# A two-layer trunk on one core: block products over neighbouring token chunks, their sums made in the first layer and kept in DRAM, and the rope of two chunks stacked

## The chip, the cores and the metric

The kernel runs on one core of one Trainium2 chip. The metric is the device time of one execution in microseconds (us). The time before is the median of three runs, 2751.1 us (2750.38 to 2755.59). One further execution was taken with the hardware profiler; the profile below is of that one.

The engines are called as the profile calls them: PE is the matrix engine (PEld its weight loads), DVE the vector engine, ACT the scalar engine, POOL the gpsimd engine, and SP the engine whose queue starts nearly all transfers. Each engine works through its own queue in order.

## The reference, cut to what matters

There are two pre-norm residual layers on 2048 tokens of width 1024. The first mixes with gated linear attention, the second with three groups of dilated windowed attention. Each layer also attends to a memory of 256 rows.

```python
h = rmsnorm(x, norm_w[i])                       # per layer
mix, q_mem, gate = gla_mixer(...) if i == 0 else dilated_mixer(...)
mem_o = memory_attention(q_mem, mem_n, w_memkv[i])
x = x + (concat([mix, mem_o]) * silu(gate)) @ w_out[i]

# dilated_mixer, layer 1: six heads of 128 in each of three groups
for g, (window, dil) in enumerate(((128, 1), (512, 4), (2048, 16))):
    qkv = (h @ w_in[:, base:base + 3 * MIXER_WIDTH]).reshape(B, T, 3, 6, 128)
    q, k = partial_rope(qkv[:, :, 0], pos), partial_rope(qkv[:, :, 1], pos)   # first 32 of 128
    o, lse = dilated_group(q, k, qkv[:, :, 2], window, dil)
o = sum over g of softmax(lse)[g] * o[g]
rest = h @ w_in[:, 9 * MIXER_WIDTH:]            # queries of the memory, gate
```

Everything is in 32-bit floats. The kernel reaches that precision with pairs of 16-bit floats, a high and a low part of each number, and three matmuls for each product (hi·hi, hi·lo, lo·hi; the helper `mm3`, L179 to L181).

## The kernel before, in words

The hidden state of the second layer, transposed, is the tile `h2T`: 128 partitions, a high and a low part, eight slices of the width, 2048 tokens. A *projection* (`proj_t`) multiplies it with 128 columns of a weight for a *chunk* of 512 tokens: 24 matmuls of 128x512 into one PSUM bank. Banks for this come in rotation from three (`mm_bank`: two of the pool ps_mm, one of ps_x). The stages, by the trace:

- **First layer, first part (0 to 458 us):** the projections and the chunked recurrence.
- **First layer, second part (458 to 906 us):** a loop over 16 blocks of 128 tokens, some 28 us each. One pass has the memory's attention, the gate and the output projection of a block (`a2_q`, `a2_gate`, `a2_out`; its results leave their banks at L683), and for the block before it the norm and its transposition into `h2T` (`a2_h2`, L697 and L698). The second layer's first weights are loaded meanwhile.
- **Pre-stage (906 to 1040 us):** twelve projections, eight for the queries of the memory (`memq`, read out at L953 to L957) and four for one part of the gate (`gate4`, read out at L999 to L1003). Between them in program order stand the loading, scaling and splitting of the first set of weights (`set_raw`, `set_norm`, `set_diff`, `set_split`; L873 to L883) and six of the eight calls of `sums`.
- **Block products (1040 to 1466 us):** twelve sets of weights. Each is multiplied by the 2x2-block scheme with seven products instead of eight (`sblock`). The token side of the 2x2 is the first half of the tokens against the second, the other side the two halves of the width. Three of the seven need sums of the four quarters of `h2T`, in the SBUF tiles S1, S2 and S4; a fourth, S3 = A11 − A21, overwrites the quarter A21 in `h2T`. Copies of A21 (`a21_d`, in DRAM) are put back at the end. `sums(x)` makes S1, S2, S4 and for x below 4 also S3 for a slice of 128 tokens of each half: L828 adds a high and a low part, L839 to L845 combine them, L832 (ACT) and L833 split the result again. The last two calls and the other four S3 run within the first set (`late`).
- **Heads (1470 to 2526 us):** 18 heads of eight steps each. A step has one projection: q or k (e even or odd) of chunk e // 2, then the scores of ten steps earlier (`att_scores`) and the products with v of thirteen steps earlier (`att_pv`). After each odd step `rope_pair` (L1127 to L1144) turns q and k of the chunk: ACT copies the 32 rows to be turned of both banks to SBUF (L1133), DVE swaps halves (L1134), POOL and DVE multiply with the tables (L1135, L1136), DVE adds them back into the banks (L1138), and ACT and DVE write the high and the low part (L1141, L1142). L1142 is the last reader of the bank. In four of each 24 steps `item_mix` (L1286 to L1300) weighs and adds the three groups of a finished head, by two multiplications on POOL (L1289, L1294) and the rest on DVE.
- **Tail (2526 to 2741 us):** the last heads, the output projection and the final norm.

A Tile scheduler puts the instructions of DVE, ACT, POOL and SP into queues, by a simulation of the program. In the second layer PE's order is the program's.

## Time and profile before

| | |
|---|---|
| median of three runs | 2751.1 us |
| the profiled execution's own time | 2743.19 us |
| its span in the trace | 2741.4 us |
| mean granted clock of PE | 0.971 |
| PE busy | 2546.4 us (93%) |
| DVE busy | 1642.0 us (60%) |
| ACT busy | 1311.6 us (48%) |
| POOL busy | 649.2 us (24%) |
| moved by DMA | 337.13 MB, mean 123 GB/s |

Busy time is the time in which an engine executes. For PE the records overlap: a matmul of 128x512 stands in the trace with some 380 ns, though the next one starts 207 ns later. A row of the groups has line, engine, operation, output and input tiles with shape and type, count, then busy time in us and mean ns of one, then idle time of the engine just before it and what ended it. A row of the waits has who waited, for which instruction, the sum in us, the count and the longest. A row of the windows has the stretch, its length, busy time and count of each engine, the granted clock of PE, and the share and rate of DMA.

### The profile page before, as it was taken

What the parts mean: (1) busy time and instruction counts of PE and PEld (TensorE: products, weight loads), DVE (VectorE), ACT (ScalarE), POOL (GpSimd) and SP (SyncE); (2) the same over time, 40 slices, a digit from 0 to 9 for tenths busy, and PEclk for the clock granted to TensorE, in tenths of its full rate; (3) what the DMA queues carried; (4) which work ended last, traced back from release to release, by engine and by line L of the source; (5) the groups of instructions that cost most, each with busy time, mean ns of one, the idle gap of its engine ahead of it and who ended that gap; (6) DMA issues with size and microseconds to landing.
All of it is one profiled execution on the core that took longest, in us unless ns stands there. A gap on an engine that the chain in (4) does not pass through costs nothing.

```text
span 2741.4 us, 45032 instructions
## 1 busy us (share of the span) xinstructions
PE 2546.4 (93%) x17137; PEld 1699.6 (62%) x17137; DVE 1642.0 (60%) x3483; ACT 1311.6 (48%) x2921; POOL 649.2 (24%) x513
## 2 busy tenths in 40 slices
PE   7989999999999959999999999799897998978899
PEld 6879998888998524544444455354453544534798
DVE  6345444655655696655655566757657576676643
ACT  6356444544444446555645455354454444535232
POOL 0000000000001254555441222423323233242200
PEclk9999999999999989999999999899998999998899
DMA  6241113342334214767754144645547446366642
GB/s 212 82 133 71 64 56 109 103 103 82 108 88 122 73 51 129 179 168 187 168 149 145 37 99 113 182 98 137 129 118 185 96 118 148 99 190 154 182 148 102
DMA packets 517837, 337.13 MB, mean 123 GB/s; under 512 B 348834, under 2 KB 460916, under 8 KB 515316
## 3 DMA queue, kind: packets, MB, share of 16 engines
q1 hardware_dynamic: 517620, 334.26, 44.5%
q8 instruction: 134, 2.20, 0.3%
q14 instruction: 83, 0.68, 0.1%
HBM read 179.45 MB, written 89.57 MB: 98 GB/s over the span
## 4 chain that ended last, share of the span: by engine, by line
PE 69%; DVE 12%; DMA 9%; issue 4%; ACT 3%; POOL 2%; SPq 1%; DVEq 0%; POOLq 0%; ACTq 0%
PE ps_mm L179 14%; PE ps_mm L180 13%; PE ps_mm L181 13%; PE ps_x L179 5%; PE ps_x L181 5%; PE ps_x L180 5%; DMA fb<-fd 3%; DMA stg<-in_w_in_b 2%; PE ps_tr L166 1%; PE ps_o L181 1%; PE ps_o L180 1%; PE ps_o L179 1%; DMA pt<-ph 1%; DVE ps_mm L1138 1%; DVE fb L1297 1%
## 5 line engine op out<-in xcount | busy, mean ns | idle before, releaser
L179 PE MATMUL ps_mm<-h2T,w 128*128 128x512 f16 x1112 | 435.7, 392 | 67.8 <-DVE q L1142 65.1
L180 PE MATMUL ps_mm<-h2T,w 128*128 128x512 f16 x1112 | 435.6, 392 | 2.7 <-POOL h2T L833 2.7
L181 PE MATMUL ps_mm<-h2T,w 128*128 128x512 f16 x1112 | 434.1, 390 | 0.0
L180 PEld LDWEIGHTS <-w 128*128 128x128 f16 x1952 | 194.2, 99 | 325.0 <-issue 124.7
L179 PE MATMUL ps_mm<-w,hT 128*128 128x256 f16 (+1 forms) x1408 | 387.5, 275 | 4.3 <-ACT v L488 1.3
L180 PE MATMUL ps_mm<-w,hT 128*128 128x256 f16 (+1 forms) x1408 | 386.4, 275 | 0.0
L181 PE MATMUL ps_mm<-w,hT 128*128 128x256 f16 (+1 forms) x1408 | 384.8, 275 | 0.4 <-DVE hT L382 0.4
L181 PEld LDWEIGHTS <-w 128*128 128x128 f16 x1952 | 194.6, 100 | 244.9 <-issue 23.7
L179 PEld LDWEIGHTS <-w 128*128 128x128 f16 x1952 | 194.4, 100 | 241.3 <-issue 19.4
L1182 ACT ACTIVATE pm<-pm,st,cols 128x256 f32<-128x256 f32 (+1 forms) x288 | 156.7, 545 | 265.1 <-DVE st L1177 260.6
L173 POOL TENSOR_TENSOR ph<-pm,ph 128x512 f16<-128x512 f32 (+2 forms) x144 | 154.8, 1075 | 481.7 <-ACT ph L172 369.4
L179 PE MATMUL ps_x<-h2T,w 128*128 128x512 f16 x552 | 211.9, 384 | 38.9 <-DVE q L1142 21.7
L173 POOL TENSOR_TENSOR stg<-mp,stg 128x512 f16<-128x512 f32 x16 | 18.5, 1159 | 834.9 <-DMA ogd<-og 459.1
L181 PE MATMUL ps_x<-h2T,w 128*128 128x512 f16 x552 | 211.7, 383 | 0.0
L180 PE MATMUL ps_x<-h2T,w 128*128 128x512 f16 x552 | 211.7, 383 | 0.0
L1173 DVE CUSTOM_DVE_ANT_0 pm<-ps_g,mw 128x256 f32<-128x256 f32 (+1 forms) x288 | 93.5, 360 | 153.1 <-PE ps_g L181 152.1
L179 PEld LDWEIGHTS <-hT 128*128 128x128 f16 x1408 | 138.8, 99 | 24.2 <-issue 5.6
L180 PEld LDWEIGHTS <-hT 128*128 128x128 f16 x1408 | 138.7, 99 | 24.2 <-issue 6.0
L1135 POOL TENSOR_TENSOR rw<-rw,rope 64x512 f32<-64x512 f32 x72 | 96.2, 1336 | 228.6 <-DVE rw L1134 210.8
L181 PEld LDWEIGHTS <-hT 128*128 128x128 f16 x1408 | 139.2, 99 | 17.8 <-DVE hT L382 0.7
L1133 ACT ACTIVATE rx<-ps_mm 32x512 f32<-32x512 f32 x96 | 56.1, 584 | 113.2 <-PE ps_mm L181 109.6
L179 PE MATMUL ps_o<-pt,v 128*128 128x128 f16 (+1 forms) x384 | 75.7, 229 | 9.7 <-DVE rw L1211 3.7
(448 smaller groups left out, 6064.9 us busy)
## 6 DMA issues: line engine op xcount, KB each, us to landing
stg<-in_w_in_b SPq DMA_DIRECT2D x80, 256.0 KB
v<-vd SPq DMA_DIRECT2D x18, 1024.0 KB
fb<-fd SPq DMA_DIRECT2D x24, 768.0 KB
od<-osb SPq DMA_DIRECT2D x68, 256.0 KB
og<-od SPq DMA_DIRECT2D x68, 256.0 KB
x<-in_x SPq DMA_DIRECT2D x32, 512.0 KB
stg<-in_w_in_b SPq DMA_DIRECT2D x24, 512.0 KB
vd<-vo SPq DMA_DIRECT2D x48, 256.0 KB
```

The lines of the kernel that those rows point to most:

```text
L166: PE.transpose(t[:, (k - k0) * P:(k - k0 + 1) * P], src[:, k * P:(k + 1) * P], ident)
L173: G.tensor_tensor(out=lo, in0=src, in1=hi, op=ALU.subtract)
L179: PE.matmul(o, sh, mh, start=first, stop=False)
L180: PE.matmul(o, sh, ml, start=False, stop=False)
L181: PE.matmul(o, sl, mh, start=False, stop=last)
L1133: A.activation(out=X[32 * j:32 * j + 32, :], in_=ts[j][0:32, :], func=AF.Copy)
L1135: G.tensor_tensor(out=W, in0=W, in1=rt[1], op=ALU.mult)
L1138: V.tensor_tensor(out=ts[j][0:32, :], in0=X[32 * j:32 * j + 32, :], in1=W[32 * j:32 * j + 32, :], op=ALU.add)
L1173: V.tensor_tensor_reduce(out=pm[:, at:at + w * P], in0=s[:, at:at + w * P], in1=masks["mw" if w == 2 else "mf"], scale=1.0, scalar=NEG, op ...
L1182: A.activation(out=p_, in_=p_, func=AF.Exp, scale=sc, bias=st[:, jc + jj:jc + jj + 1], accum_out=st[:, ns + jc + jj:ns + jc + jj + 1])
L1297: V.tensor_tensor(out=acc, in0=acc, in1=fb[:, 2], op=ALU.add)
```

## The change

There are three parts.

**Neighbouring chunks.** The token side of the 2x2 is now chunk c against chunk c + 1 (512 tokens each) for c = 0 and 2, in place of the first half against the second. The tiles S1, S2, S4 are laid out by slices of 128 tokens, so that a product that uses them reads four runs of 128 for its 512 columns.

**Sums in the first layer.** With this pairing a slice of sums needs blocks b and b + 4 of 128 tokens, and can be made while the first layer still runs. `a2_sums` does so after the blocks in `SUMS_AT` for six of the eight slices, S3 too, and stores them in DRAM (`s_d`). One call has three instructions on POOL, ten on DVE, four on ACT and four transfers of 256 KB. The last call has one buffer for its four outputs, the others four. In the pre-stage `load_s` and `load_s3` bring them back (6 MB together) on SP's queue, and only the sums 6 and 7 are made there; the first set has none. The order of the twelve projections changes to chunks 1, 3, 0, 2 for the memory and 1, 3, 0, 2 for the gate.

**Rope of two chunks.** `evac` writes high and low parts of all 128 rows out of a bank without the turn, after copying its 32 rows into a quarter of the SBUF tile `rx`; after that the bank is free. When both chunks of a pair (0 and 2, then 1 and 3) are there, `rope_quad` does swap, multiplications, addition and split for all four quarters at once (128x512 in place of 64x512), and eight DVE copies of 32x512 put the turned rows over the others in q and k. It runs 36 times where `rope_pair` ran 72 times.

```diff
+SUMS_AT = (6, 8, 10, 12, 13, 14)
...
+        def a2_sums(i):
+            b = i // 4 * 8 + i % 4
+            (h11, l11), (h12, l12), (h21, l21), (h22, l22) = (
+                [h2T[:, hl, 4 * k:4 * k + 4, d * P:(d + 1) * P] for hl in range(2)] for d in (b, b + 4) for k in (0, 1))
...
+            def split(t, name, o, eng):
+                o = o.rearrange("p a (k n) -> p a k n", k=4)
+                A.activation(out=o[:, 0], in_=t, func=AF.Copy)
+                eng.tensor_tensor(out=o[:, 1], in0=t, in1=o[:, 0], op=ALU.subtract)
+                SY.dma_start(s_d[name][:, i], o)
+
+            G.tensor_tensor(out=x, in0=h21, in1=l21, op=ALU.add)
+            V.tensor_tensor(out=s, in0=h22, in1=l22, op=ALU.add)
+            V.tensor_tensor(out=s, in0=s, in1=x, op=ALU.add)
+            os_ = [ag[:, 3]] * 3 if i + 1 == len(SUMS_AT) else [as_[:, y] for y in (1, 2, 3)]
+            split(s, "S1", os_[0], V)
+            G.tensor_tensor(out=x, in0=h11, in1=x, op=ALU.subtract)
+            G.tensor_tensor(out=x, in0=x, in1=l11, op=ALU.add)
+            split(x, "S3", os_[1], V)
+            V.tensor_tensor(out=s, in0=s, in1=h11, op=ALU.subtract)
+            V.tensor_tensor(out=s, in0=s, in1=l11, op=ALU.subtract)
+            split(s, "S2", os_[2], V)
+            V.tensor_tensor(out=s, in0=h12, in1=s, op=ALU.subtract)
+            V.tensor_tensor(out=s, in0=s, in1=l12, op=ALU.add)
+            split(s, "S4", ag[:, 3], V)
...
             if b > 0:
                 a2_h2(b - 1, xt)
+                if b in SUMS_AT:
+                    a2_sums(SUMS_AT.index(b))
...
-        def quad(i, k, hl, ts):
-            return h2T[:, hl, 4 * k:4 * k + 4, i * H + ts.start:i * H + ts.stop]
+        def quad(i, k, hl, x, n=1):
+            t0 = x // 4 * 1024 + i * 512 + x % 4 * P
+            return h2T[:, hl, 4 * k:4 * k + 4, t0:t0 + n * P]
...
-                    mm3(o, wt[:, 0, k], wt[:, 1, k], hi[:, k], lo[:, k], k == 0, k == 3)
+                    if an in ops:
+                        mv, ov_ = [quad(*ops[an], x, cc * 4, 4)[:, k] for x in range(2)], o
+                    else:
+                        mv, ov_ = [Ss[an][:, cc * 4:cc * 4 + 4, x, k] for x in range(2)], o.rearrange(
+                            "p (a n) -> p a n", a=4)
+                    mm3(ov_, wt[:, 0, k], wt[:, 1, k], *mv, k == 0, k == 3)
...
-        memq(2)
-        out_q(0, 0, proj_t(wq["w"][0], 0))
+        load_s(slice(0, 4))
+        memq(1)
+        out_q(3, 0, proj_t(wq["w"][0], 3))
...
-        gate4(2)
-        sums(0)
-        sums(1)
-        gate4(0)
-        sums(2)
-        memq(1)
+        gate4(1)
+        for x in range(4):
+            load_s3(x)
+        gate4(3)
+        load_s(slice(4, 6))
+        for x in range(4, 6):
+            load_s3(x)
+        sums(6)
+        memq(0)
...
-    def rope_pair(ts, c, g, dsts):
+    def evac(ts, c, g, dsts, X):
         r0 = 64 * (c // 2)
         for j in range(2):
-            A.activation(out=X[32 * j:32 * j + 32, :], in_=ts[j][0:32, :], func=AF.Copy)
-        V.stream_shuffle(W, X, SWAP)
-        G.tensor_tensor(out=W, in0=W, in1=rt[1], op=ALU.mult)
-        V.tensor_tensor(out=X, in0=X, in1=rt[0], op=ALU.mult)
-        for j in range(2):
-            V.tensor_tensor(out=ts[j][0:32, :], in0=X[32 * j:32 * j + 32, :], in1=W[32 * j:32 * j + 32, :], op=ALU.add)
+            A.activation(out=X[r0 + 32 * j:r0 + 32 * j + 32, :], in_=ts[j][0:32, :], func=AF.Copy)
         for j in range(2):
             hi = gdst(dsts[j][:, 0, :], g, c)
             A.activation(out=hi, in_=perm(ts[j], g), func=AF.Copy, scale=SQ)
             V.scalar_tensor_tensor(out=gdst(dsts[j][:, 1, :], g, c), in0=perm(ts[j], g), scalar=SQ, in1=hi,
                                    op0=ALU.mult, op1=ALU.subtract)
+
+    def rope_quad(c, g, dsts, X):
+        cs = slice(c * 512, (c + 1) * 512)
+        W = tl(bk, [P, 512], F32, "rw")
+        V.stream_shuffle(W, X, SWAP)
+        G.tensor_tensor(out=W, in0=W, in1=rope[1][:, cs], op=ALU.mult)
+        V.tensor_tensor(out=X, in0=X, in1=rope[0][:, cs], op=ALU.mult)
+        V.tensor_tensor(out=W, in0=X, in1=W, op=ALU.add)
+        hl = X.bitcast(F16).rearrange("p (a n) -> p a n", a=2)
+        hi, lo = fold(hl[:, 0], g), fold(hl[:, 1], g)
+        A.activation(out=hi, in_=perm(W, g), func=AF.Copy, scale=SQ)
+        V.scalar_tensor_tensor(out=lo, in0=perm(W, g), scalar=SQ, in1=hi, op0=ALU.mult, op1=ALU.subtract)
+        for y in range(2):
+            for j in range(2):
+                r0 = 64 * y + 32 * j
+                for x in range(2):
+                    V.tensor_copy(gdst(dsts[j][0:32, x, :], g, c + 2 * y), fold(hl[r0:r0 + 32, x], g))
...
-        live[e % 2] = proj_t(d["w"][e % 2], e // 2)
+        c = (0, 2, 1, 3)[e // 2]
+        live[e % 2] = proj_t(d["w"][e % 2], c)
...
+        if e % 4 == 3:
+            rope_quad(c % 2, u[1], hds[n]["qk"], rx)
```

How the scheduler's queues change shows at three places. The numbers behind a tile's name tell its instances apart.

The first is DVE's queue at one mixing step of the heads. Before (rx and rw are the rope's tiles, fb and og the mixing's, osb a finished part of the attention's output, q and k the heads' operands, ps_x and ps_mm the projections' banks):

```order
L1134 STREAM_SHUFFLE rw_18712<-rx_18711 64x512
L1211 COPY osb_18749<-ps_o_18679 128x512
L1177 TENSOR_SCALAR st_2642_18307<-mx_18725,cols_88 128x2
L1136 TENSOR_TENSOR rx_18711<-rx_18711,rope_2382_16404 64x512
L1138 TENSOR_TENSOR ps_x_18625<-rx_18711,rw_18712 32x512
L1138 TENSOR_TENSOR ps_mm_18686<-rx_18711,rw_18712 32x512
L1291 TENSOR_TENSOR fb_18932<-og_18928,fb_18932 128x512
L1142 SCALAR_TENSOR_TENSOR q_18208<-ps_x_18625,q_18208 128x4x128
L1142 SCALAR_TENSOR_TENSOR k_18209<-ps_mm_18686,k_18209 128x4x128
L1297 TENSOR_TENSOR fb_18932<-fb_18932 128x512
```

After, at a mixing step of the same head (L1175 is the low part out of the bank, L1181 the rope's swap, L1341 to L1350 the mixing, L1223 the maxima of the scores):

```order
L1175 SCALAR_TENSOR_TENSOR q_18208<-ps_x_18621,q_18208 128x4x128
L1341 TENSOR_TENSOR fb_18654<-og_18650,fb_18654 128x512
L1347 TENSOR_TENSOR fb_18654<-fb_18654 128x512
L1348 TENSOR_TENSOR fb_18654<-fb_18654 128x512
L1223 ISA pm_18730,mx_18729<-ps_g_18728,mw_16386 128x128
L1223 ISA mx_18729 128x1
L1223 ISA pm_18730,mx_18729<-ps_g_18728,mw_16386 128x128
L1223 ISA mx_18729 128x1
L1181 STREAM_SHUFFLE rw_18713<-rx_18514 128x512
L1261 COPY osb_18753<-ps_o_18675 128x512
L1350 TENSOR_TENSOR sg_18648<-fb_18654,sg_18648 128x16x32
L1175 SCALAR_TENSOR_TENSOR k_18209<-ps_mm_18682,k_18209 128x4x128
```

The bank of q is now read out ahead of the mixing and with no rope ahead of it; the bank of k is read out ten instructions later, behind the mixing.

The second is DVE's queue in the last block of the first layer. Before (x is the block's output, ps_o and ps_x its banks, h2T the transposed hidden state):

```order
L683 SCALAR_TENSOR_TENSOR x_10909<-ps_o_10911,cj_10907,x_10909 128x256
L683 SCALAR_TENSOR_TENSOR x_10909<-ps_x_10962,cj_10907,x_10909 128x256
L698 TENSOR_TENSOR h2T_5111<-ps_tr_11022,h2T_5111 128x4x128
L774 CAST rb_1512_11232<-rm_11230 128x1
L698 TENSOR_TENSOR h2T_5111<-ps_tr_11029,h2T_5111 128x4x128
L683 SCALAR_TENSOR_TENSOR x_10909<-ps_o_10911,cj_10907,x_10909 128x256
L683 SCALAR_TENSOR_TENSOR x_10909<-ps_x_10962,cj_10907,x_10909 128x256
L692 SCALAR_TENSOR_TENSOR sg_11044<-x_10909,rs_1486_11041,nwb_850_5121 128x1024
```

After, with the last call of `a2_sums` (L719 takes the low part of a split, L730 to L734 combine; stg is the staging tile in which the sums lie):

```order
L687 SCALAR_TENSOR_TENSOR x_11011<-ps_o_11013,cj_11009,x_11011 128x256
L731 TENSOR_TENSOR stg_5333<-stg_5333,h2T_5115 128x512
L687 SCALAR_TENSOR_TENSOR x_11011<-ps_x_11064,cj_11009,x_11011 128x256
L702 TENSOR_TENSOR h2T_5115<-ps_tr_11131,h2T_5115 128x4x128
L719 TENSOR_TENSOR stg_5333<-stg_5333 128x512
L812 CAST rb_1488_11337<-rm_11335 128x1
L719 TENSOR_TENSOR stg_5333<-stg_5333 128x512
L733 TENSOR_TENSOR stg_5333<-h2T_5115,stg_5333 128x512
L734 TENSOR_TENSOR stg_5333<-stg_5333,h2T_5115 128x512
L687 SCALAR_TENSOR_TENSOR x_11011<-ps_o_11013,cj_11009,x_11011 128x256
L719 TENSOR_TENSOR stg_5333<-stg_5333 128x512
L687 SCALAR_TENSOR_TENSOR x_11011<-ps_x_11064,cj_11009,x_11011 128x256
```

The sums' instructions stand between those that let PE's banks go.

The third is DVE's queue in the pre-stage, between the two DVE readers of one bank of `gate4`. Before, the end of that stretch up to the second reader, L1003; the first, L999, stands seven rows above these (w are split weights, c scratch, S the sums):

```order
L883 SCALAR_TENSOR_TENSOR w_11467<-c_1550_11503,ws_11475,w_11467 128x512
L883 SCALAR_TENSOR_TENSOR w_11563<-c_1551_11505,ws_11475,w_11563 128x512
L1052 TENSOR_SCALAR cols_88<-cols_88 128x1
L842 TENSOR_TENSOR c_1546_11483<-c_1546_11483,c_1547_11488 128x512
L883 SCALAR_TENSOR_TENSOR w_11680<-c_1552_11507,ws_11475,w_11680 128x512
L883 SCALAR_TENSOR_TENSOR w_11685<-stg_11245,ws_11475,w_11685 128x512
L833 TENSOR_TENSOR S_1492_11094<-c_1533_11387,S_1492_11094 128x4x128
L1003 SCALAR_TENSOR_TENSOR c_1555_11535<-ps_x_11509,cols_88,c_1554_11534 128x512
```

After (L1044 and L1048 are the bank's readers, L925 a split of weights, L877 and L872 belong to `sums`):

```order
L1044 TENSOR_SCALAR c_1522_11614<-ps_x_11589,cols_88 128x512
L1095 TENSOR_SCALAR cols_88<-cols_88 128x1
L925 SCALAR_TENSOR_TENSOR w_11726<-stg_11350,ws_11555,w_11726 128x512
L877 TENSOR_TENSOR c_1518_11571<-c_1518_11571,c_1517_11569 128x512
L925 SCALAR_TENSOR_TENSOR w_11626<-c_1515_11565,ws_11555,w_11626 128x512
L925 SCALAR_TENSOR_TENSOR w_11726<-c_1516_11567,ws_11555,w_11726 128x512
L872 TENSOR_TENSOR S_1466_11194<-c_1518_11571,S_1466_11194 128x512
L1048 SCALAR_TENSOR_TENSOR c_1523_11615<-ps_x_11589,cols_88,c_1522_11614 128x512
```

Thirteen instructions stood between the two readers of a bank at the latest place; now six do.

More of the change, by code (lines that the diff above doesn't have):

```diff
@@ L628, in trunk @@
         V.tensor_tensor(out=bmix, in0=bv, in1=bmix, op=ALU.max)
+        mhs = ((stg, "stg"), (sga, "stg"))
         def a2_q(b):
@@ L636, in a2_q @@
             om = tl(k1, [P, 256], F32, "om")
-            mem_pv(mem0, mem_scores(mem0, mem_T(qm, k2), k2, ("mp", "mpt"), ((stg, "stg"), (sga, "stg"))), om, ps_g)
+            mem_pv(mem0, mem_scores(mem0, mem_T(qm, k2), k2, ("mp", "mpt"), mhs), om, ps_g)
             return hT, om
@@ L711, in trunk @@
             V.tensor_copy(iwo[:, j:j + 1], wo[j][1])
+        as_ = tl(stg, [P, 4, 2, 512], F16, "stg")
+        ag = tl(sga, [P, 4, 2, 512], F16, "stg")
+        mhs = (as_[:, 0], ag[:, 0])
         gt = a2_gate(hT)
@@ L892, in product @@
                 wt = w[COMBOS[i]]
-                hi, lo = (quad(*ops[an], x, ts) if an in ops else Ss[an][:, x, :, ts] for x in range(2))
                 for k in range(4):
-                    mm3(o, wt[:, 0, k], wt[:, 1, k], hi[:, k], lo[:, k], k == 0, k == 3)
+                    if an in ops:
[4 more added lines that the diff above has]
+                    mm3(ov_, wt[:, 0, k], wt[:, 1, k], *mv, k == 0, k == 3)
                 return o
@@ L1021, in trunk @@
         cur = set_raw(sets[0][2])
-        out_q(0, 1, proj_t(wq["w"][1], 0))
-        gate4(2)
-        sums(0)
-        sums(1)
-        gate4(0)
-        sums(2)
-        memq(1)
+        out_q(3, 1, proj_t(wq["w"][1], 3))
+        gate4(1)
[7 more added lines that the diff above has]
+        memq(0)
         set_norm(cur, ps_g)
-        sums(3)
         for x in ("T1", "T2", "T3", "T4"):
             set_diff(cur, x)
-        gate4(1)
-        sums(4)
+        sums(7)
+        gate4(0)
         for x in range(4):
             set_split(cur)
-        memq(3)
-        sums(5)
-        gate4(3)
+        memq(2)
+        gate4(2)
         for x in range(3):
             set_split(cur)
-        late = [lambda x=x: sums(x) for x in (6, 7)]
-        for x in range(4, 8):
-            ts = slice(x * P, (x + 1) * P)
-            late.append(lambda ts=ts: diff(ts, f32q(0, 0, ts, V), f32q(1, 0, ts, V)))
         nxt = set_raw(sets[1][2])
@@ L1057, in side @@
                 def side(i):
-                    if late:
-                        late.pop(0)()
                     if cc == 0 and i == 5:
```

60 lines of the change are left out of this document (32 added, 28 removed).

## The prediction

> **What bounds the kernel now.** I read the windows by stage first, since the stages have different limits.
>
> ```profile
> core 0: us, PE busy (x) PEld busy (x) DVE busy (x) ACT busy (x) POOL busy (x), PEclk, DMA share, GB/s
> 540.00:860.00 320.00, 318.61 (x3054) 287.45 (x3053) 185.31 (x428) 141.49 (x309) 27.27 (x24) 1.00 0.34 94
> 906.00:1040.00 134.00, 98.26 (x426) 42.95 (x425) 112.63 (x136) 60.49 (x103) 69.16 (x46) 0.89 0.21 63
> 1040.00:1466.00 426.00, 423.25 (x2254) 205.93 (x2253) 253.14 (x445) 250.58 (x485) 197.75 (x149) 1.00 0.65 163
> 1590.00:2510.00 920.00, 830.93 (x4869) 434.99 (x4868) 613.61 (x1432) 433.75 (x1023) 291.94 (x232) 0.95 0.52 133
> ```
>
> TensorE (PE) is full in the block loop that ends the first layer (540 to 860) and in the block products (1040 to 1466). It has holes in the pre-stage (134 − 98.3 = 35.7 us) and in the heads (920 − 830.9 = 89.1 us), and the granted clock is lower in just these two. The waits of PE over the whole span name what ended the holes:
>
> ```profile
> PE ps_mm L179 <- DVE q L1142: 65.1, 19, 7.4
> PE ps_x L179 <- DVE q L1142: 21.7, 12, 4.1
> PE ps_x L179 <- DVE c L1003: 15.0, 2, 13.4
> PE ps_x L179 <- DVE c L899: 13.5, 1, 13.5
> ```
>
> In the heads a projection waits for a PSUM bank whose last reader is L1142, the end of the rope (65.1 + 21.7 = 86.8 us). In the pre-stage two waits of over 13 us are for a bank whose last reader is a late DVE instruction. Next I looked at what follows such a hole, with windows laid over four of them (the first two in the heads, the next two in the pre-stage) and over full work:
>
> ```profile
> 1714.90:1721.70 6.80, 5.92 (x14) 2.02 (x14) 5.58 (x11) 2.68 (x8) 4.59 (x4) 0.50 0.41 124
> 2465.80:2476.00 10.20, 5.19 (x13) 1.90 (x13) 5.62 (x11) 3.68 (x8) 1.35 (x2) 0.50 0.34 72
> 970.80:984.50 13.70, 5.64 (x14) 2.05 (x14) 13.59 (x18) 6.76 (x13) 6.37 (x5) 0.50 0.36 115
> 1015.20:1028.80 13.60, 5.26 (x13) 1.95 (x14) 13.59 (x13) 5.14 (x8) 11.08 (x7) 0.50 0.24 57
> 925.00:931.00 6.00, 6.00 (x29) 2.73 (x28) 1.38 (x2) 2.19 (x5) 0.00 (x0) 1.00 0.66 221
> ```
>
> At full clock 29 matmuls take 6.00 us, 0.207 us each, so one projection (24 matmuls) is 5.0 us. At clock 0.50 fourteen took 5.92 us, 0.42 each. So a hole costs itself and then slow work. By the mean clocks, (1 − 0.95) × 920 = 46 us of speed are lost in the heads and (1 − 0.89) × 134 = 15 in the pre-stage. Part of the half clock lies in holes and costs nothing: in the four windows PE was busy for 22.0 of 44.3 us. Weighted by stage (heads 11.1 of 17.0, pre-stage 10.9 of 27.3) the cost of slow matmuls is 46 × 0.65 = 30 us in the heads and 15 × 0.40 = 6 in the pre-stage. The timeline of one hole in the heads shows its making:
>
> ```profile
> 1920.60 1.97 POOL L1289 TENSOR_TENSOR fb<-og,fb 128x512 f32<-128x512 f32 x1 [1.92 <-DMA fb<-fd]
> 1921.40 1.72 DVE L1138 TENSOR_TENSOR ps_mm<-rx,rw 32x512 f32<-32x512 f32 x1
> 1922.53 1.96 POOL L1294 TENSOR_TENSOR fb<-og,fb 128x512 f32<-128x512 f32 x1
> 1923.14 1.89 DVE L1138 TENSOR_TENSOR ps_x<-rx,rw 32x512 f32<-32x512 f32 x1
> 1925.07 1.28 DVE L1297 TENSOR_TENSOR fb<-fb 128x512 f32<-128x512 f32 x1
> 1926.27 0.68 DVE L1142 SCALAR_TENSOR_TENSOR q<-ps_mm,q 128x512 f16<-128x512 f32 x1
> 1927.00 0.58 PE L179 MATMUL ps_mm<-h2T,w 128*128 128x512 f16 x1 [4.46 <-DVE q L1142]
> ```
>
> The mixing of heads (L1289 to L1297) runs on POOL and DVE just while the rope is on DVE. The rope's additions take 1.72 and 1.89 us there, and the mixing's L1297 stands ahead of L1142 in DVE's queue. The bank comes free 4.46 us late.
>
> **The rope.** Before, a pair of projections holds two banks through the following chain; the groups by line and form give durations:
>
> ```profile
> L1134 DVE STREAM_SHUFFLE rw<-rx 64x512 f32<-64x512 f32 x72 | 51.9, 720 | 1.0
> L1135 POOL TENSOR_TENSOR rw<-rw,rope 64x512 f32<-64x512 f32 x72 | 96.2, 1336 | 228.6 <-DVE rw L1134 210.8 <-DVE st L1177 17.8
> L1136 DVE TENSOR_TENSOR rx<-rx,rope 64x512 f32<-64x512 f32 x72 | 59.2, 822 | 1.2
> L1138 DVE TENSOR_TENSOR ps_mm<-rx,rw 32x512 f32<-32x512 f32 x96 | 74.6, 777 | 9.5 <-POOL rw L1135 4.6 <-DVE rx L1136 0.5 <-DVE st L1177 0.2
> L1141 ACT ACTIVATE q<-ps_mm 128x512 f16<-128x512 f32 x48 | 28.2, 587 | 48.1 <-DVE ps_mm L1138 48.1
> L1142 DVE SCALAR_TENSOR_TENSOR q<-ps_mm,q 128x512 f16<-128x512 f32 x48 | 33.1, 689 | 7.1 <-ACT q L1141 6.2
> ```
>
> Bank held at best: copy 0.59 (an ACT copy, as L1141), shuffle 0.72, POOL 1.34, addition 0.78, ACT 0.59, DVE 0.69: 4.7 us and more for the second bank. After, the bank is let go after two ACT copies and one DVE instruction, 0.59 + 0.59 + 0.69 = 1.9 us, with no POOL step. DVE work for two chunks was 2 × 0.72 + 2 × 0.82 + 4 × 0.78 + 4 × 0.69 = 9.0 us. It becomes 4 × 0.69 + 0.72 + 0.82 + an addition 0.78 + 0.69 + eight f16 copies of 32x512. No row has such a copy from SBUF; the nearest bounds are these:
>
> ```profile
> L245 DVE COPY qmT<-ps_tr x16: 418/424/425, 455.2 to 868.5; 128x512 f16<-128x512 f16 x16
> ```
>
> 0.42 us (f16, but from PSUM) is my value and near the top; downward I allow half of it. Eight copies are 1.7 to 3.4 us and the sum 7.5 to 9.2 us, 36 times. I take no change in DVE's load; at the top it is 36 × 0.2 = 7 us on an engine busy for 613.6 of 920, hidden by its idle third. The Trainium skill (VectorE: DVE Perf Modes, the perf-mode tier table) rates 16-bit copies within SBUF at four times the base rate and those from PSUM at twice at most. By that rule the copy would take half of L245's 0.42, which makes the sum 7.5 us, 36 × 1.7 = 61 us less DVE work than by the row; no run here shows such a copy, and the time would be the same, since DVE is not the bound. POOL has 36 instructions where it had 72 (−48 us, idle anyway). ACT gains 36 × 0.59 = 21 us on 433.75 of 920, hidden.
>
> The new addition waits for POOL's multiply, 1.34 us and up to 2 beside the mixing; behind it on DVE stand the scores' maxima and the next banks' readers. That is the old wait at half the number, and the banks of its own pair are free by then.
>
> What is late next: one of the two banks. In the new DVE order at a mixing step q's reader stands ahead of the mixing, but k's behind ten instructions (L1341 to L1350), two of which wait for POOL. I price those ten at L1297's contended 1.28 twice, 0.7 to 1.9 for the other long ones and POOL's two 1.96: 6 to 10 us, against the 5.0 us of the next projection plus 1 to 2 us of scores. About 20 mixing steps lie in the window; the residue is 0 to 3 us each, and I take 1.3: 26 us with its clock (range 10 to 65). The rope's result comes later too, by some 4 us (eight copies and the second multiply's queue), but scores start two projections (over 10 us) after the last one. Heads: −(86.8 + 30) + 26 = **−91 us**.
>
> **Sums out of the pre-stage.** Its DVE is busy for 112.6 of 134 us, and the timeline shows the bank's reader behind weight splits slowed by POOL:
>
> ```profile
> 971.47 3.20 DVE L883 SCALAR_TENSOR_TENSOR w<-c,ws,w 128x512 f16<-128x512 f32 x2
> 974.65 1.57 DVE L842 TENSOR_TENSOR c<-c,c 128x512 f32<-128x512 f32 x1
> 978.07 0.74 DVE L1003 SCALAR_TENSOR_TENSOR c<-ps_x,cols,c 128x512 f32<-128x512 f32 x1
> ```
>
> Four of six `sums` leave: per call eight DVE instructions, three to four on POOL, three to four on ACT, by these rows:
>
> ```profile
> L833 DVE TENSOR_TENSOR S<-c,S 128x512 f16<-128x512 f32 x24 | 24.9, 1041 | 0.0
> L828 DVE TENSOR_TENSOR c<-h2T 128x512 f32<-128x512 f16 x24 | 21.9, 931 | 0.0
> L828 POOL TENSOR_TENSOR c<-h2T 128x512 f32<-128x512 f16 x16 | 21.0, 1319 | 53.4 <-DVE sg L692 29.8 <-DMA qmd<-c 9.0 <-DMA sgd<-c 7.0
> ```
>
> That is 4 × 8 × about 0.98 = 31 us of DVE, leaving 82, less than PE's own 98.3 − 6 = 92. So the holes should go but for a residue (0 to 20, I take 7): the first set's weights must still be split before 1040. The new loads, 6 MB, bounded by the 221 GB/s of the row 925:931 at 27 us, run on SP's queue ahead of the raw weights of the first set: 1.5 MB, 7 us, covered by the projections. The loads over A21 wait on SP until two gate projections have read it; behind them on SP are stores of later projections, which nobody reads before the block products, and the second set's weights, due a whole set (426/12 = 35 us) after the first's. −(35.7 + 6) + 7 = **−35 us**. The two sums that move out of the first set of block products gain nothing: PE is full there.
>
> **Sums into the first layer.** Six calls, in iterations of about 28 us (16 blocks from 458 to 906) in which PE is full and DVE 185.3/320 = 58% busy. A call adds ten DVE instructions (six like L828, four like L833): 6 × 0.93 + 4 × 1.04 = 9.7 us; if POOL always ran beside them, by the longer of these two, up to 16:
>
> ```profile
> 955.38 1.64 DVE L828 TENSOR_TENSOR c<-h2T 128x512 f32<-128x512 f16 x1
> 1000.06 0.68 DVE L828 TENSOR_TENSOR c<-h2T 128x512 f32<-128x512 f16 x1
> ```
>
> 28 × 0.58 + 9.7 = 25.9 us: just under the iteration. The readers of PE's banks (L683, now L687) come to stand between these instructions, each wait 1 or 2 us at most against the pipelining of one block: 3 us over five calls (0 to 20). The last call is worse: its outputs share one buffer, so ACT and DVE stand until each DMA has landed. No row has that landing; the nearest is a 1 MB load, issued and then ready 4.7 us later:
>
> ```profile
> 924.88 0.93 SPq L860 DMA_DIRECT2D stg<-in_w_in_b  x2
> 929.55 1.06 ACT L114 ACTIVATE w<-stg 128x1024 bf16<-128x1024 f32 x1 [3.60 <-DMA stg<-in_w_in_b]
> ```
>
> Three landings of 2 to 4.7 us hold ACT for 6 to 14 us in the last blocks; behind its waiting copy stand the copies of blocks 14 and 15 out of PSUM, and the third projection now needs block 15 at once. Part is covered by two projections (10 us): +7 (3 to 15). Together **+10 us**.
>
> **Moving operand in four runs.** S products read four runs of 128 instead of one of 512. Two runs of 64 are in the trace:
>
> ```profile
> L284 PE MATMUL ps_g<-vm,mp x64: 216/220/220, 467.8 to 881.8; 128*128 128x128 f16 x64
> ```
>
> 220 ns is less than two of the 0.207 us intervals would give, and it is a pipelined record, so I take no cost.
>
> **Sum.** −91 − 35 + 10 = −116. The profiled execution took 2743.2 us (span 2741.4 and 1.8 around it), so 2627; the median of the runs, 2751.1, is 7.9 above it, so **2635 us**.
>
> **Rivals.** (1) *The queue keeps half.* Most holes in the heads come back as k's bank waiting behind the mixing (or for ACT), at 3 us and with half clock: −50 in the heads, 2676 us. For: the order; 26 waits now. Against: no POOL step is left between projection and bank. The Trainium skill (SBUF, who interferes with whom) says that a two-port copy on DVE and a POOL instruction shut each other out entirely; the eight copies would then wait for POOL, as this rival has it. No row has that pair; the contended 1.64 against 0.68 is of a two-input instruction. By rows: 288 copies × 1 us × POOL's 32% = 92 us more of DVE, 77% busy. (2) *Everything goes:* no residue, sums free: 2751.1 − 117 − 42 = 2592. (3) *The change does not do what it says in the heads:* banks stay as late; only −35 + 10 is left: 2726. (4) *Slower:* strided runs double the S products. 12 weight sets × 2 chunk pairs × 3 products × 12 matmuls = 864, × 0.207 = +179 on a stage in which PE is 423.25 of 426 busy; with −116, 2814. It decides from 116/864 = 0.13 us a matmul. Against: L284's row.
>
> **Chances.** Forecast 0.47, (1) 0.28, (2) 0.12, (3) 0.06, (4) 0.05, and 0.02 for a part of (4)'s price that leaves the time within 0.2%, about what a measurement of this kernel can tell from no change. The forecast's own range, from the residues (heads 10 to 65, pre-stage 0 to 20, first layer 3 to 35), is about 2610 to 2675, since not all come at one end. It reaches on to (1) above and to part of (2) below: 2585 to 2690. Cases (3), (4) and the lowest of (2) stay outside, less than 0.2. Faster is the forecast with (1), (2) and (3), 0.93; same 0.02; slower 0.05.
>
> **What would show it.** Right: PE's waits for L1142's successor under 40 us and for the pre-stage's bank under 10; clock 0.98 or more in the heads; the block loop still over 98% busy. Wrong: waits on k's reader at 3 us or more (1); ps_o or ps_x waits on L687 in the block loop (sums mispriced); a mean S matmul over 500 ns (4).

## The result, and the profile after

The changed kernel takes 2675.4 us (median of four runs, 2673.8 to 2676.7), the kernel before 2753.4 (median of four). The ratio is 0.9717, with a 95% interval of 0.9700 to 0.9734. The forecast was 2635 with a range of 2585 to 2690: the sign and the range hold, the gain is 78 us instead of 116. The forecast's own range ended at about 2675; the time lies at that end, and the part of the range above it was there for rival (1).

The stages have moved, so I cut both traces at the same matmuls: the first row is the loop of the first layer from the end of block 0 to the end of block 14, then the last block with the first four projections, the rest of the pre-stage with the block products, the 18 heads, and the tail. The columns are those of the windows in the prediction. Before:

```profile
516.40:888.60 372.20, 370.22 (x3557) 333.93 (x3554) 218.25 (x503) 165.41 (x364) 33.42 (x29) 1.00 0.36 99
888.60:924.70 36.10, 34.27 (x218) 21.58 (x219) 18.54 (x34) 15.49 (x30) 4.52 (x4) 1.00 0.30 91
924.70:1477.20 552.50, 514.01 (x2639) 244.99 (x2637) 361.57 (x577) 310.01 (x585) 264.93 (x192) 0.97 0.56 142
1477.10:2491.40 1014.30, 924.81 (x5333) 477.65 (x5332) 659.30 (x1536) 472.58 (x1105) 309.09 (x245) 0.95 0.49 125
2491.40:2741.40 250.00, 222.06 (x1455) 192.22 (x1451) 124.29 (x233) 81.22 (x193) 28.70 (x19) 0.95 0.51 151
```

After:

```profile
517.90:894.90 377.00, 371.30 (x3557) 333.53 (x3554) 256.88 (x553) 175.78 (x384) 52.52 (x44) 1.00 0.39 112
894.90:937.90 43.00, 38.46 (x218) 23.39 (x219) 25.92 (x44) 18.13 (x34) 6.59 (x5) 0.88 0.54 179
937.90:1455.00 517.10, 508.29 (x2639) 243.87 (x2637) 303.81 (x520) 295.83 (x560) 227.42 (x170) 1.00 0.62 157
1454.80:2420.40 965.60, 908.05 (x5333) 474.85 (x5332) 638.33 (x1638) 505.06 (x1143) 241.12 (x209) 0.98 0.52 131
2420.40:2674.70 254.30, 221.05 (x1455) 191.28 (x1451) 124.95 (x240) 81.02 (x193) 26.46 (x19) 0.94 0.49 150
```

The counts of PE in each pair of rows agree, so the lengths can be subtracted: +4.8, +6.9, −35.4, −48.7, +4.3. With 1.5 us ahead of the first row that is the difference of the two spans, 2741.4 − 2674.7 = 66.7. (The changed kernel's profiled execution was 1 us above its median; the one of before was 8 to 10 below. So the traces show 67 of the 78 us, and the sizes by stage are those of these two executions.) In the heads PE's own busy time fell by 16.8 us, as its clock rose from 0.95 to 0.98, and its idle time by 31.9, from 89.5 to 57.6. So most of the idle time in the heads is still there, but PE's waits give it other names:

```profile
PE ps_o L180 <- DVE osb L1261: 43.0, 18, 6.1
PE ps_g L181 <- DVE k L1193: 14.1, 5, 3.5
...
PE ps_g L180 <- DVE k L1193: 1.6, 2, 0.8
```

No wait for a projection's bank is left in the heads. PE now waits for the bank of the attention's output, ps_o, which L1261 copies out on DVE, and for the rope's last copies into q and k (L1193), without which the scores can't start. The timeline of the longest of these waits has DVE's rows from the end of its standing to the copy, and PE's first row after it:

```profile
2218.11 1.02 DVE L1341 TENSOR_TENSOR fb<-og,fb 128x512 f32<-128x512 f32 x1 [6.49 <-DMA fb<-fd]
2219.05 0.67 DVE L1175 SCALAR_TENSOR_TENSOR q<-ps_mm,q 128x512 f16<-128x512 f32 x1
...
2221.63 0.68 DVE L1347 TENSOR_TENSOR fb<-fb 128x512 f32<-128x512 f32 x1
...
2223.41 1.28 DVE L829 SCALAR_TENSOR_TENSOR w<-stg,ws,w 128x1024 f16<-128x1024 f32 x1
...
2224.68 1.91 DVE L1350 TENSOR_TENSOR sg<-fb,sg 128x512 f32<-128x512 f32 x1
...
2228.25 0.68 DVE L1261 COPY osb<-ps_o 128x512 f32<-128x512 f32 x1
...
2228.99 0.27 PE L180 MATMUL ps_o<-pt,v 128*128 128x128 f16 x1 [6.13 <-DVE osb L1261]
```

DVE stood idle for 6.49 us until the transfer of fb (the weights of the three groups) had landed, because L1341 was next in its queue. Then all that had collected behind it went first, the rest of the mixing and two weight splits (L829) among it, and PE had waited 6.13 us when L1261 was through. Over the heads DVE stood like this for 40.0 us:

```profile
DVE fb L1341 <- DMA fb<-fd: 40.0, 10, 6.5
```

### The profile page after: what moved, and what is told of

Its sections match the earlier page's. It is cut to its first block, busy times and chain, and to the rows that moved or that the text cites. A ratio compares the mean times of both kernels' runs of the same rounds, so it can differ in the third digit from the quotient of the medians.

```text
span 2674.7 us, 45223 instructions
## 1 busy us (share of the span) xinstructions
PE 2532.0 (95%) x17137; PEld 1698.7 (64%) x17137; DVE 1610.2 (60%) x3595; ACT 1342.8 (50%) x2957; POOL 562.6 (21%) x471
## 5 line engine op out<-in xcount | busy, mean ns | idle before, releaser
L180 PE MATMUL ps_mm<-h2T,w 128*128 128x512 f16 x1112 | 426.9, 384 | 1.2 <-ACT c L947 1.2
L181 PE MATMUL ps_mm<-h2T,w 128*128 128x512 f16 x1112 | 426.1, 383 | 0.0
L182 PE MATMUL ps_mm<-h2T,w 128*128 128x512 f16 x1112 | 426.0, 383 | 0.0
L174 POOL TENSOR_TENSOR ph<-pm,ph 128x512 f16<-128x512 f32 (+2 forms) x144 | 144.9, 1006 | 615.2 <-ACT ph L173 429.9
L1223 DVE CUSTOM_DVE_ANT_0 pm<-ps_g,mw 128x256 f32<-128x256 f32 (+1 forms) x288 | 93.5, 360 | 99.1 <-PE ps_g L182 98.2
L181 PE MATMUL ps_g<-k,q 128*128 128x256 f16 (+1 forms) x288 | 69.3, 249 | 14.1 <-DVE k L1193 14.1
```

Source lines behind the costliest of these rows:

```text
L174: G.tensor_tensor(out=lo, in0=src, in1=hi, op=ALU.subtract)
L180: PE.matmul(o, sh, mh, start=first, stop=False)
L181: PE.matmul(o, sh, ml, start=False, stop=False)
L182: PE.matmul(o, sl, mh, start=False, stop=last)
L1223: V.tensor_tensor_reduce(out=pm[:, at:at + w * P], in0=s[:, at:at + w * P], in1=masks["mw" if w == 2 else "mf"], scale=1.0, scalar=NEG, op ...
```

## The experiments

The theory from here on, **Q**: the heads lose their time because DVE's queue stands for fb and the bank's reader stands behind it. The rival, **L**: a mixing step holds more DVE work than it has room for, whatever stands where. (A queue *stands for* what its next instruction waits for.) Ratios are against the kernel before on the same chip; the changed kernel had 0.9717. What lies ahead of the heads differed by up to 15 us between runs whose instructions are the same there, so for the heads I compare their own stretch of 5333 matmuls, from the first projection to the last.

**Loads two steps earlier.**

```diff
-            y, z = divmod(x - 3, step)
+            y, z = divmod(x - (1 if h < 4 else 3), step)
             if 0 <= y < 4 and z == 0:
                 items[y] = (item_og(h, y), item_fb(h, y))
```

> The loads of the mixing (sg, og, fb) are started two steps earlier for heads 0 to 3, the mixing itself stays where it is. Theory Q (the heads lose their time because DVE's queue stands at the mixing's first multiplication, L1341, until the DMA of fb has landed, and the copy out of the bank of the attention's output, L1261, stands behind it): DVE's waits for fb (40.0 us) fall under 10, PE's waits for L1261 (43.0 us) fall under 15, and the time goes from 2675 to 2630 to 2650. Theory L (a mixing step simply holds more DVE work than a step has room for, so waiting or not makes no difference): PE's waits for L1261 stay above 30 and the time stays within 10 us of 2675.

Measured: 2673.8 us, ratio 0.9723 (0.9709 to 0.9738), waits 39.9 (L1261) and 38.2 (fb). By the letter this is what L said. But the queues show that the edit moved nothing: the loads of fb are issued at 1867.20, 1882.85 and 1898.27 us, as before right behind the mixing that sets their buffer free. The scheduler takes what is ready by its simulation and not by the program's place. So it had started the loads as early as the buffer allows, and it has the mixings 13 to 22 us apart on DVE where the program has them four steps apart. The run doesn't tell the theories apart.

**The copy on ACT.**

```diff
-            V.tensor_copy(osb, ob)
+            A.activation(out=osb, in_=ob, func=AF.Copy)
```

> The copy of the attention's output out of its bank (L1261) is on ACT instead of DVE: ACT gains 72 copies of about 0.6 us. Theory Q and theory L both have the copy late because of DVE's queue: PE's waits for it fall from 43.0 us to under 10, the time to 2630 to 2650. A third theory, B (the one bank of ps_o is too few, whoever empties it): the waits stay above 25 us, now for ACT, and the time within 15 us of 2675.

Measured: 2682.6 us, ratio 0.9761 (0.9745 to 0.9777), slower than without the edit. The wait is as long, now for ACT, and the trace shows ACT standing for DVE and DVE for fb, longer than before (68.1 us over the heads instead of 40.0):

```profile
PE ps_o L180 <- ACT osb L1261: 50.9, 19, 6.2
```

```profile
1884.90 1.02 DVE L1341 TENSOR_TENSOR fb<-og,fb 128x512 f32<-128x512 f32 x1 [7.41 <-DMA fb<-fd]
...
1891.04 2.19 ACT L828 ACTIVATE w<-stg,ws 128x1024 f16<-128x1024 f32 x2 [10.16 <-DVE ws L818]
...
1896.18 0.59 ACT L1261 ACTIVATE osb<-ps_o 128x512 f32<-128x512 f32 x1
```

Theory B's numbers came out (a wait above 25 us, time within 15), though the rows give another reason: a second in-order queue that depends on the first stands with it. (The run with the mixing held, below, has the same single bank and hardly waits for it.) My expectation for Q had overlooked that.

**One part at a time.** The kernel before with `evac`, `rope_quad` and their loop; then the changed kernel with `rope_pair` and its loop.

```diff
+        c = (0, 2, 1, 3)[e // 2]
...
-            rope_pair([live[0], live[1]], e // 2, u[1], hds[n]["qk"])
+            evac([live[0], live[1]], c, u[1], hds[n]["qk"], rx)
...
+            rope_quad(c % 2, u[1], hds[n]["qk"], rx)
```

> The kernel before with the new rope alone: no sums in the first layer, the old pairing of the chunks. If the parts add up, as the profiles say (heads -49, tail +4): 45 us under the kernel before, about 2708. If the sums' part has a share in the heads' gain or loss (loads or clock carried over): more than 15 us away from that.

> The changed kernel with the old rope: sums in the first layer and the pairing of neighbouring chunks alone. If the parts add up, as the profiles say (first layer and first projections +13, then -35): 22 to 30 us under the kernel before, about 2726. If the strided reading of S1, S2, S4 or the DRAM traffic costs anything in the block products, the stretch from the fourth projection to the end of the block products is above 517 us.

Measured: the rope alone 2699.4 us, ratio 0.9817 (0.9803 to 0.9832), 50 us under the kernel before; the sums alone 2720.4, ratio 0.9890 (0.9875 to 0.9906), 29 under. The product of the ratios is 0.971. The heads take 963.5 us with the new rope alone (965.6 in the changed kernel) and 1013.1 with the old one (1014.3 in the kernel before), so what stands ahead of them changes little. With the sums alone the stretch from the fourth projection (937.6) to the end of the block products (1453.2) is 515.6 us: reading S1, S2 and S4 in four runs costs nothing that shows. The records of the matmuls that read them have a mean of 379 ns in the block products, as in the kernel before.

**The mixing held at its step.** Its first DVE multiplication takes a factor 1 made from the maximum of that step's scores, so it can't be queued sooner.

```diff
+                one = tl(sp, [P, 1], F32, "one")
+                V.tensor_scalar(out=one, in0=hds["mx"][:, 0:1], scalar1=0.0, scalar2=1.0, op0=ALU.mult, op1=ALU.add)
+                item_mix(*items.pop(y), pin=one)
...
-        V.tensor_tensor(out=fb[:, 0], in0=o0.rearrange("p (l q) -> p q l", q=16),
-                        in1=fb[:, 0], op=ALU.mult)
+        V.scalar_tensor_tensor(out=fb[:, 0], in0=o0.rearrange("p (l q) -> p q l", q=16), scalar=pin,
+                               in1=fb[:, 0], op0=ALU.mult, op1=ALU.mult)
```

> The first DVE multiplication of the mixing (heads 0 to 3) takes a factor of 1 that is made from the scores' maximum of the step at which the mixing stands in the program, so that the scheduler can't put it into DVE's queue before that step; the loads stay early. The run with earlier loads had left the queues as they were: in both, four mixings stand 13 to 22 us apart in DVE's queue, though the program has them four steps (some 27 us) apart, each as soon as the scheduler thinks that fb has landed. Theory Q (DVE stands for fb, and PE's bank of the attention's output stands behind DVE): DVE's waits for fb go from 40.0 us to under 8, PE's waits for that bank from 43.0 to under 15, heads 25 to 45 us shorter, 2630 to 2650. Theory L (too much DVE work in a mixing step): the waits for the bank stay above 30, and the time within 10 us of 2675.

Measured: **2627.1 us**, ratio 0.9567 (0.9543 to 0.9591), the fastest version here, 48 us under the changed kernel by the medians and 1.5% by the ratios. DVE's and PE's waits and the heads:

```profile
DVE fb L1342 <- DMA fb<-fd: 0.6, 1, 0.6
```

```profile
PE ps_g L181 <- DVE k L1193: 8.3, 5, 2.3
PE ps_o L180 <- DVE osb L1262: 6.3, 3, 3.8
```

```profile
1464.70:2366.30 901.60, 887.96 (x5334) 469.46 (x5333) 608.10 (x1650) 501.57 (x1136) 238.62 (x208) 1.00 0.56 139
```

The stretch is 64 us shorter than 965.6 with one small instruction more in a mixing step, and the clock is full. L is out for the stacked rope: it had the waits for the bank above 30 us, and they are 6.3, though no instruction was taken away. The standing of Q is shown as a cause, but not as the whole 64 us. The time came out under Q's range, the heads' gain above its 25 to 45 us, and the edit did more than end the standing. Most of the mixings are now 24 to 27 us apart, and DVE's busy time in the heads fell by 30 us, from 638 to 608. More than half of that, 17 us, is in the rope's eight copies (105.0 to 87.8 us): of the 288, only 11 took over 0.6 us, where 29 had. How the 64 us divide between less standing and less DVE time was not separated.

**Two steps later.** The same edit with `x - 7` for `x - 5`.

> As the run before, but two steps later, so that the mixing comes between two turns of the rope (e = 2 and 6) instead of right behind one. If the scores' waits for the rope's last copies (14.1 + 1.6 us) come from POOL's multiplications of the mixing running beside these copies (theory C: a copy beside POOL took 0.9 to 1.5 us, alone 0.28): they go from 15.7 to under 5 here and stay in the run before, and this run is 5 to 20 us faster than that one. If they come from the length of the rope's chain alone, they stay above 10 in both, and the two runs are within 8 us.

Measured: 2662.0 us, ratio 0.9685 (0.9658 to 0.9713), slower than the run before. The scores' waits did fall, to 1.6 us, but a wait took their place that I hadn't foreseen: POOL's two multiplications were not held, stand for fb in POOL's queue, and the rope's multiplication (L1182) stands behind them. PE waited 24.1 us for L1262 and 18.9 us for transfers of the attention's weights (pt).

```profile
POOL fb L1340 <- DMA fb<-fd: 72.8, 15, 10.2
```

```profile
DVE rw L1184 <- POOL rw L1182: 59.1, 16, 6.3
```

For theory C the run is not clean: the scores' waits fell as it said, but they fell by about half in the run before too (8.6 us).

**The rope not stacked.** Banks let go early as in the change, but swap, multiplications, addition and split for each pair of projections (64 rows, 72 times).

```diff
+            evac([live[0], live[1]], c, u[1], hds[n]["qk"], rx)
+            rope_half(c, u[1], hds[n]["qk"], rx)
...
-        if e % 4 == 3:
-            rope_quad(c % 2, u[1], hds[n]["qk"], rx)
```

> The rope for each pair of projections by itself (64 rows, 72 times), not stacked, but with the banks let go early as in the changed kernel. DVE gets 36 more swaps, multiplications, additions and splits, some 110 us of work, POOL 36 multiplications. If the early release of the banks is what gained in the heads, the time stays within 20 us of 2675. If the stacking, that is DVE's load, is what counts: 40 us or more above.

Measured: 2719.5 us, ratio 0.9902 (0.9878 to 0.9926), 44 above the changed kernel and the same as with the old rope. PE's waits and the heads:

```profile
PE ps_o L180 <- DVE osb L1261: 90.1, 36, 6.1
```

```profile
1454.20:2465.30 1011.10, 919.47 (x5334) 479.14 (x5333) 769.21 (x1821) 538.28 (x1173) 300.31 (x244) 0.96 0.49 125
```

Letting the banks go early without stacking gains nothing to speak of, 1011.1 against 1013.1, but it also brings 110 us more DVE work than the old rope had (769 against 659). With 769 us in place of the changed kernel's 638 the wait stands at ps_o, and twice as long.

**Four sums in the first layer.** `SUMS_AT = (6, 8, 10, 12)`, and `sums(4)`, `sums(5)` in the pre-stage in place of their loads.

> Only four of the six calls of sums in the first layer; the slices 4 and 5, whose blocks are the last to be made, go to the pre-stage with 6 and 7. If the last call with its one buffer, and the one before it, cost what the fourth projection is late (937.9 against 924.7 in the kernel before): the fourth projection ends at 925 to 930 here. The pre-stage then has 16 more DVE instructions, 15 us: if its DVE has that room, the time is 5 to 10 us under 2675; if not, the stretch from the fourth projection to the end of the block products grows from 517 by 10 or more and the time is 2670 to 2685.

Measured: 2672.2 us, ratio 0.9732 (0.9707 to 0.9757), no change that can be told. The last block ends 19.6 us after block 14 (23.4 with six calls, 17.2 before), so the last two calls do cost some 4 us there; the fourth projection ends at 934.2, not at 925 to 930. The stretch after it is 526.3 us instead of 517.1, and PE waits 10.4 us for a bank that DVE empties late. What is taken off one end comes back at the other.

**Held, with the other ropes.** The edit of the run that was fastest, on the old rope and on the one not stacked.

> The run with the old rope (sums in the first layer alone, 2720) with the mixing held at its step on DVE, as in the run that held it (2627). If DVE's standing for fb was also what made the old holes (a bank whose last reader, the rope's end, came late at mixing steps): PE's waits for that reader fall from some 87 us to under 40 and the time to 2660 to 2690. If the old holes came from the length of the old rope's chain beside the mixing: the time stays above 2705.

> The run with the rope for each pair and the early release (2719) with the mixing held at its step. Without holding it, the early release alone was worth nothing: 2719 against 2720 for the old rope. If its 90 us of waits for the attention's bank were DVE's standing for fb: they fall under 30 and the time to 2640 to 2665, so that stacking is worth only 15 to 40 us. If they come from DVE's own load (110 us more than stacked): they stay above 60 and the time stays above 2690.

Measured: 2715.1 us, ratio 0.9880 (0.9861 to 0.9900), and 2717.3, ratio 0.9894 (0.9879 to 0.9909). PE's waits in the first and in the second:

```profile
PE ps_mm L180 <- DVE q L1183: 54.7, 27, 4.9
PE ps_x L180 <- DVE q L1183: 26.4, 17, 5.0
```

```profile
PE ps_o L180 <- DVE osb L1262: 65.8, 27, 5.8
```

With the old rope the 87 us of waits only fell to 81, and without stacking 65.8 are left, so by their numbers both runs say what their second case said: the old rope's chain, and DVE's load. But a new wait has come in. DVE no longer stands for fb in the heads (21.1 and 26.2 us without holding), yet it now stands for the rope's multiplication on POOL, which at the mixing steps comes behind the mixing's two products there. With the old rope that is 35.3 us where it was 6.9 (the larger of the two rows is below), without stacking 17.8 us where there was none; with the stacked rope it was 3.7.

```profile
DVE ps_mm L1179 <- POOL rw L1176: 33.0, 13, 3.9
```

What is measured is that the two gains need each other; how much of what is left belongs to the chain itself, to DVE's load and to POOL's queue stays open. In the heads' own stretch: old rope 1013.1, held 1005.2; early release without stacking 1011.1, held 988.1; stacked 965.6, held 901.6.

**Held on POOL too.** One column of fb is multiplied by the factor ahead of POOL's two, at the step and two steps later.

```diff
+            G.tensor_tensor(out=fb[:, 1:3, 0, 0], in0=fb[:, 1:3, 0, 0], in1=pin, op=ALU.mult)
```

> The changed kernel with the mixing held at its step on POOL too (a multiplication by 1 of one column of fb ahead of POOL's two). In the run with DVE alone held, POOL still stood for fb, 37.1 us, but DVE waited for POOL's rope step only 3.7 us. So there is little left to gain: 2618 to 2632, the same as with DVE alone held.

> The same, two steps later. With DVE alone held there (2662), DVE waited 59.1 us for POOL's rope step, which stood behind POOL's mixing and its fb. If that was all that made the later place slower: these waits fall under 10, the scores' waits stay under 5, and the time is at or under that of the run before, 2610 to 2632. If the later place is bad for another reason (the mixing between two turns of the rope delays the second turn): above 2645.

Measured: 2649.5 us, ratio 0.9648 (0.9633 to 0.9662), and 2657.9, ratio 0.9679 (0.9665 to 0.9694). The first expectation is missed. In the second run DVE's waits for the rope's step are gone and the scores' waits are 3.0 us, as its first case said, but the time is that of its second case, above 2645. DVE no longer waits for the rope's step on POOL, but now for the mixing's, and PE for ps_o; the rows are of the first and of the second:

```profile
DVE fb L1350 <- POOL fb L1342: 9.7, 7, 1.4
...
PE ps_o L180 <- DVE osb L1262: 29.2, 17, 6.2
```

```profile
DVE fb L1350 <- POOL fb L1342: 25.0, 19, 1.4
...
PE ps_o L180 <- DVE osb L1262: 38.3, 19, 5.8
```

With DVE alone held, POOL had done its two products before DVE came to the mixing, and the first sum (there L1348) took 801 ns on the mean. Held on both it starts while POOL works and takes 1396 and 1773 ns, after waiting for POOL. The edit has a price of its own too: the multiplication of one column took 1.02 us of POOL on the mean, 20 times, ahead of POOL's products. In this kernel it was better to hold only the engine that others wait for and let the idle one run ahead. How the 22 and 31 us divide was not tried.

## Why the prediction was half right

**Sums out of the pre-stage: −35 forecast, −35.4 measured.** The two holes of over 13 us are gone (the longest wait left there is 3.0), PE's idle time in the stretch fell from 38.5 to 8.8 us, the clock there is 1.00 in place of 0.97, and DVE's work in that stretch fell from 361.6 to 303.8 us.

**Sums into the first layer: +10 forecast (3 and 7), +11.7 measured (4.8 and 6.9).** The block loop gives up little, and the last block with the third projection, which waits for it, pays the rest.

**Four runs for one: nothing forecast, nothing found.** PE is busy for 508.3 us of 517.1 in the stretch of the block products, with as many matmuls as before, and the records of those that read S have a mean of 379 ns before and after. The ground in the prediction was thin, though: L284's record of 220 ns has 128 columns, and the 0.207 us that it was held against is the interval of matmuls of 512.

**The rope's DVE work: no change forecast, −7 us measured.** The rope's own rows in the heads add up to 322 us before and 315 after. (All DVE work there fell by 21 us, 659.3 to 638.3.) The copy that no row had shown takes 0.28 us by its median, between my two ends of 0.21 and 0.42. The tier rule that the prediction named from the Trainium skill (VectorE: DVE Perf Modes, the perf-mode tier table) would have had the lower end; the trace lies a third above it.

**The heads: −91 forecast, −48.7 measured.** The whole of the potential was 117 us, and the old bank waits did go, all of them. The step that failed is "What is late next: one of the two banks", with its residue of 26 us (range 10 to 65); what came back is 68 us, above the range. I had followed the projections' banks only, and found k's reader ten instructions back. But the same rows of DVE's order show `L1261 COPY osb` behind the mixing, and ps_o is one bank, which PE needs every other step, while the projections have three. And I priced the ten instructions by their work and by POOL, not by the DMA that the first of them waits for, though that wait stood in the trace of before, in the heads, behind the longer waits for the banks:

```profile
DVE fb L1291 <- DMA fb<-fd: 21.4, 14, 3.7
```

The run with the mixing held shows the size: there the heads lose 113 us of 1014, all but 4 of the potential. What else that edit moved, the mixings' spacing and 30 us of DVE time, is in these 113 us as well.

All the signs that the prediction had named for being right came out: no wait for the successor of L1142, 4.6 us at the pre-stage's bank, a clock of 0.98 in the heads, and PE busy for 98.5% of the block loop. None of them looked at ps_o in the heads.

**Rival (1) had the size, not the place.** It gave −50 in the heads and 2676 us; but no time is lost at k's bank, so that its number came out is luck. Its copies beside POOL are real, at a smaller price: 29 of the 288 took over 0.6 us, 35 us together, or 27 us more than at 0.28 each, where the rival had 92.

**The scores' slack.** "Scores start two projections (over 10 us) after the last one" was said to cover the longer chain. It did not in seven places, 15.7 us together. Five of them, 14.1 us, end right behind a copy that took 1.5 us instead of 0.28 beside POOL.

**The tail: nothing forecast, +4.3 us.** PE waits there for a split of the output projection's operand (14.8 us over four waits after, 10.3 over three before). It goes with the rope: the tail's 1455 matmuls take 252.9 us with the rope alone and 246.9 with the sums alone, against 250.0 before. Why stays open.

## What to carry to other kernels

When a wait goes, look for what is late next among all readers in the queue of the engine that was late, and at the buffer with the fewest copies first, not at the successor of the old wait. A transfer's wait at the head of an in-order queue is paid by everything behind it; a scheduler that expects the transfer to have landed by then can put it there. Moving the one behind it to another engine that depends on the first did not help here; a data dependence that held the waiting instruction back did. Releasing the banks early was worth 2 us while the releasing engine's work grew by 110, 49 when it didn't grow, and 113 with the mixing held as well.

## What the runs showed of the hardware

A DVE copy of 16-bit numbers within SBUF was held up by a POOL instruction that ran beside it until that one ended. DVE's and POOL's rows of the changed kernel:

```profile
1706.46 0.28 DVE L1193 COPY k<-rx 32x512 f16<-32x512 f16 x1
...
1707.18 0.88 DVE L1193 COPY q<-rx 32x512 f16<-32x512 f16 x1
1708.08 1.50 DVE L1193 COPY k<-rx 32x512 f16<-32x512 f16 x1
1709.61 0.28 DVE L1193 COPY q<-rx 32x512 f16<-32x512 f16 x1
```

```profile
1706.66 1.26 POOL L1339 TENSOR_TENSOR fb<-og,fb 128x512 f32<-128x512 f32 x1 [2.33 <-DMA fb<-fd]
1707.88 1.56 POOL L1344 TENSOR_TENSOR fb<-og,fb 128x512 f32<-128x512 f32 x1
```

Each of the two long copies ends 0.14 us behind the end of a POOL instruction; alone the same copy takes 0.28. It is so for all 29 long copies (0.13 to 0.15 us behind), and none of the 259 others, at most 0.29 us each, overlaps a POOL instruction by more than 0.16 us. The Trainium skill (SBUF — State Buffer, "Who interferes with whom") says that a two-port copy on DVE and a POOL instruction lock each other out for a whole instruction. The trace agrees on the side of the copies: 0.88 and 1.50 us against 0.28.
